# The scan's clamped decay differences: one subtraction on VectorE and one rectifier on ScalarE, or eight rectifiers with a bias on ScalarE

## The chip, the cores and the metric

One core of a Trainium2 chip runs the whole kernel. Times are device microseconds of that core; the median of the runs counts. TensorE multiplies matrices into PSUM, VectorE, ScalarE and GpSimd work element by element, and each engine works through a queue of its own in order. SyncE issues most of the DMAs.

## The reference

One step of a two-layer streaming encoder over 1024 prompt tokens and 32 sample tokens: first a Mamba-2 layer (SSD), then a latent attention layer, each followed by a gated per-layer embedding. What the change touches is in the scan of the first layer:

```python
Acs = jnp.cumsum(dt * A, axis=2)
seg = Acs[:, :, :, None] - Acs[:, :, None, :]
Lmat = jnp.exp(jnp.where(tri, seg, -jnp.inf))
CB = jnp.einsum('bclgn,bcsgn->bclsg', Cm, Bm)
M = CB[..., None] * Lmat * dt[:, :, None]
y_diag = jnp.einsum('bclsgr,bcsgrp->bclgrp', M, x)
```

`A` is negative, so `Acs` falls within a chunk, and `seg` is at most 0 wherever `tri` lets it through. There are 32 heads in 8 groups of 4.

## The kernel before, in words

The first layer (`phase_ssd`) goes by the 8 groups of heads. For each group six blocks of 128 columns of the input weights are multiplied with the normalised input (`mblock`, L311; the matmuls themselves are at L215 in `gemm`, with results in three PSUM buffers `mm`). The results go to SBUF through ScalarE (L327) or VectorE (L329), are convolved (L461 on ScalarE, three steps L463 on VectorE), and pass a SiLU (L188, L189). Every matrix is split into a high and a low part, so a product is three matmuls; ScalarE (L204) and GpSimd (L205) split the weights.

`scan_group` (L475) then runs over a group's tokens in five steps `q`: four quarters of the prompt with two chunks of 128 tokens each (the kernel uses chunks of 128, not 64), and the sample with one of 32. In a step:

- SyncE loads `ex` (L492): the running sums of four heads along the columns, the same on all partitions, [128, 4 heads, 256]. `ex` has two buffers. `eb` is loaded likewise (L495).
- TensorE transposes x and B into the PSUM tiles `trx` and `trb` (L500 to L502) and multiplies C and B into the other half of `trb` (L505). Each has one buffer.
- VectorE forms `xe` (L512) and `xd` (L518), ScalarE empties B out of `trb` into `bt` (L514), TensorE forms the chunk states `st` (L517), VectorE masks the products of C and B into `cbm` (L520), which lets `trb` go.
- The decays: VectorE subtracts from `ex` each row token's own sum `tok(32)` (L524), ScalarE forms max(0, -x) (L525) and exp(-x) (L526), VectorE multiplies with `cbm` (L527).
- VectorE and GpSimd carry the state `hT` from chunk to chunk (L535, L538, L540; three buffers), TensorE multiplies it with C into `yf` (L546) and `ex` with `xd` into `yd` (L553), and VectorE adds these up (L559 to L562) and adds the skip term (L566). The last state of the prompt and that of the sample are stored by ScalarE's queue (L488, L568).

`gate` (L467) multiplies the result of the group before with its gate on GpSimd (L473), `finish` (L570) normalises and stores it; the loop from L605 on writes scan, blocks and gates of neighbouring groups one after another. The order on the engines is not this one: the kernel is built under `tile.TileContext(nc, schedule_with_timeline_sim=True)` (L1522), a planner that orders every engine's queue at compile time by its own estimates of when each instruction can run, and that also sets the waits. So matmuls of a scan stand in between those of the next group's blocks.

Of the kernel before, what the change touches and what calls it, by code (L numbers as in the profile page):

```python
# [12 lines left out]
AF = mybir.ActivationFunctionType  # L13
ALU = mybir.AluOpType
# [158 lines left out]
def bc_last(ap, n):  # L173
    return ap.unsqueeze(len(ap.shape)).to_broadcast(list(ap.shape) + [n])
# [96 lines left out]
def phase_ssd(c, ctx):  # L271
    nc, tc, I, O = c.nc, c.tc, c.I, c.O
# [202 lines left out]
    def scan_group(g, S):  # L475
# [5 lines left out]
        for q in range(5):  # L481
            chs = (2 * q, 2 * q + 1) if q < 4 else (8,)
            nc_, L = (2, 128) if q < 4 else (1, 32)
# [7 lines left out]
            ex = wk.tile([P, 4, 256], F32, tag="ex", name="ex", bufs=2)[:L, :, :W]  # L491
# [15 lines left out]
            def tok(a):  # L507
                return tokT[:L, chs[0] : chs[0] + nc_, a + 4 * g : a + 4 * g + 4]
# [11 lines left out]
            nc.vector.tensor_tensor(cbm.rearrange("p (c l) -> p c l", c=nc_), trb[:L, :nc_, 128 : 128 + L],  # L520
                                    bc_mid(c.tri[:L, :L], nc_), op=ALU.mult)

            dv = ex.rearrange("p h (c l) -> p h c l", c=nc_)
            nc.vector.tensor_tensor(dv, dv, bc_last(tok(32).rearrange("p c h -> p h c"), L), op=ALU.subtract)  # L524
            nc.scalar.activation(ex, ex, AF.Relu, scale=-1.0)  # L525
            nc.scalar.activation(ex, ex, AF.Exp, scale=-1.0)  # L526
            nc.vector.tensor_tensor(ex, ex, bc_mid(cbm, 4), op=ALU.mult)  # L527
            yd = pc.tile([P, 2, 256], F32, tag="yd", name="yd")
# [76 lines left out]
    for g in range(G):  # L605
        scan_group(g, Ss[g])
        if g + 1 < G:
            bc_blocks(g + 1)
        if g:
            gate(g - 1, 0, Ss[g - 1])  # L610
            gate(g - 1, 1, Ss[g - 1])
        if g + 1 < G:
            x_block(g + 1, 0)
        else:
            gate(g, 0, Ss[g])
        if g:
            finish(g - 1, Ss[g - 1])
        if g + 1 < G:
            x_block(g + 1, 1)
        else:  # L620
            up = up_product(c, 0, (0, T), lambda: kp.tile([P, T1], F32, tag="cx", name="upr", bufs=6),
                            lambda: kp.tile([P, 3 + T1], F32R, tag="raw", name="upx", bufs=RAWB),
                            lambda: mm.tile([P, 512], F32, tag="mm", name="mm"),
                            lambda: kp.tile([P, T1], F32, tag="cx", name="upe", bufs=6), 4)
            next(up)
            gate(g, 1, Ss[g])
            finish(g, Ss[g])
# [908 lines left out]
```

## Time and profile before

| what | value |
|---|---|
| median of three runs | 2018.41 us (2017.17 to 2023.32) |
| the profiled execution's own time | 2016.99 us |
| its span from first to last instruction | 2015.2 us |
| mean granted TensorE clock | 0.992 of full speed (2.4 GHz) |
| TensorE, VectorE, ScalarE, GpSimd busy | 1931.1, 1301.3, 1003.1, 962.7 us |

The profile is of one execution. Busy time is the time in which an engine works on instructions; PE is TensorE's matmuls, PEld its weight loads, DVE VectorE, ACT ScalarE, POOL GpSimd, SPq the queue of SyncE's DMAs. "L524" is a line of the kernel. "[4.58 <-DVE ex L524]" behind an instruction says that its engine sat idle for 4.58 us just before it, and which instruction's end was the last that it waited for.

### The profile page before, as it was taken

What the parts mean: (1) busy time and instruction counts of PE and PEld (TensorE: products, weight loads), DVE (VectorE), ACT (ScalarE), POOL (GpSimd) and SP (SyncE); (2) the same over time, 40 slices, a digit from 0 to 9 for tenths busy, and PEclk for the clock granted to TensorE, in tenths of its full rate; (3) what the DMA queues carried; (4) which work ended last, traced back from release to release, by engine and by line L of the source; (5) the groups of instructions that cost most, each with busy time, mean ns of one, the idle gap of its engine ahead of it and who ended that gap; (6) DMA issues with size and microseconds to landing.
All of it is one profiled execution on the core that took longest, in us unless ns stands there. A gap on an engine that the chain in (4) does not pass through costs nothing. (4 is left out here: it accounts for less than half of the span.)

```text
span 2015.2 us, 32636 instructions
## 1 busy us (share of the span) xinstructions
PE 1931.1 (96%) x12867; PEld 1772.6 (88%) x12867; DVE 1301.3 (65%) x1646; ACT 1003.1 (50%) x1707; POOL 962.7 (48%) x811
## 2 busy tenths in 40 slices
PE   8999999999999998999998999999999999999999
PEld 6989899998999998999998899777778777779999
DVE  6889886758567675444267534264688787986444
ACT  4435444353444447333243441577687867754331
POOL 5543534343443444455678443122545453645773
PEclk9999999999999999999999999999999999999999
DMA  4133433324233336544333312433512221315432
GB/s 140 53 89 86 93 95 94 84 84 100 68 93 90 78 109 218 177 149 152 95 119 116 95 60 77 164 108 97 114 46 71 57 64 37 107 58 192 128 123 76
DMA packets 110730, 204.27 MB, mean 101 GB/s; under 512 B 18224, under 2 KB 60720, under 8 KB 110448
## 3 DMA queue, kind: packets, MB, share of 16 engines
q1 hardware_dynamic: 105472, 193.17, 32.7%
q0 software_dynamic: 2800, 6.91, 1.8%
q8 instruction: 101, 1.65, 0.3%
q10 hardware_dynamic: 2304, 2.10, 0.3%
q14 instruction: 53, 0.43, 0.1%
HBM read 156.81 MB, written 38.83 MB: 97 GB/s over the span
## 5 line engine op out<-in xcount | busy, mean ns | idle before, releaser
L205 POOL TENSOR_TENSOR wl<-wraw,wh 128x1024 fp32r<-128x1024 f32 (+2 forms) x185 | 376.4, 2036 | 459.9 <-ACT wh L204 416.9
L215 PE MATMUL mm<-hh,wh 128*128 128x384 f32 (+2 forms) x1152 | 376.9, 328 | 2.3 <-ACT xr L375 1.4
L215 PE MATMUL mm<-hh,wl 128*128 128x384 f32 (+2 forms) x1152 | 377.7, 328 | 0.0
L215 PE MATMUL mm<-hl,wh 128*128 128x384 f32 (+2 forms) x1152 | 376.1, 327 | 0.0
L204 ACT ACTIVATE wh<-wraw 128x1024 fp32r<-128x1024 f32 (+2 forms) x182 | 157.7, 866 | 265.8 <-PE pso L215 109.7
L215 PE MATMUL pso<-yhl,wh 128*128 128x264 f32 x1536 | 283.5, 285 | 5.9 <-DVE yhl L229 3.0
L215 PEld LDWEIGHTS pso<-yhl,wh 128*128 128x128 f32 x1536 | 239.6, 189 | 7.5 <-DVE yhl L229 4.0
L215 PE MATMUL pso<-yhl,wl 128*128 128x264 f32 x768 | 219.0, 285 | 2.5 <-POOL wl L205 2.5
L215 PEld LDWEIGHTS mm<-hh,wh 128*128 128x128 f32 (+1 forms) x1152 | 216.7, 188 | 5.3 <-ACT xr L375 1.7
L215 PEld LDWEIGHTS mm<-hh,wl 128*128 128x128 f32 (+1 forms) x1152 | 216.8, 188 | 4.2 <-issue 2.8
L215 PEld LDWEIGHTS mm<-hl,wh 128*128 128x128 f32 (+1 forms) x1152 | 216.9, 188 | 0.9 <-issue 0.2
L215 PE MATMUL psi<-yhl,wh 128*128 128x264 f32 (+1 forms) x896 | 166.2, 286 | 4.2 <-ACT yhl L228 3.9
L463 DVE SCALAR_TENSOR_TENSOR cx<-raw,pv,cx 128x1060 f32<-128x1060 f32 x96 | 141.7, 1480 | 39.3 <-ACT cx L461 38.6
L215 PEld LDWEIGHTS pso<-yhl,wl 128*128 128x128 f32 x768 | 145.1, 189 | 3.0 <-POOL wl L205 3.0
L215 PE MATMUL pg<-hH,wl 128*128 128x264 f32 x512 | 145.9, 285 | 0.6 <-POOL wl L205 0.6
L215 PE MATMUL pg<-hH,wh 128*128 128x264 f32 x512 | 145.9, 285 | 0.0
L215 PE MATMUL pg<-hL,wh 128*128 128x264 f32 x512 | 145.6, 285 | 0.0
L215 PEld LDWEIGHTS psi<-yhl,wh 128*128 128x128 f32 (+1 forms) x896 | 137.4, 184 | 5.9 <-ACT yhl L228 4.1
L1288 PE MATMUL st<-qk 128*128 128x512 f32 (+2 forms) x576 | 140.0, 358 | 1.2 <-DMA qk<-mr 0.5
L1309 POOL TENSOR_TENSOR pl<-pf,ph 128x512 fp32r<-128x512 f32 x64 | 81.5, 1273 | 106.8 <-DVE ph L1308 98.3
L215 PE MATMUL psi<-yhl,wl 128*128 128x264 f32 (+1 forms) x448 | 129.2, 288 | 1.6 <-POOL wl L205 1.6
L538 POOL TENSOR_TENSOR hm<-hT,cd_all 128x256 f32<-128x256 f32 x64 | 55.0, 859 | 136.5 <-DVE hT L540 83.3
(525 smaller groups left out, 4605.7 us busy)
## 6 DMA issues: line engine op xcount, KB each, us to landing
wraw<-in_inW SPq DMA_DIRECT2D x48, 512.0 KB, 3.5
ex<-acs_d SPq DMA_DIRECT2D x32, 512.0 KB, 5.3
wraw<-in_outW SPq DMA_DIRECT2D x32, 512.0 KB, 3.7
yraw<-y_d SPq DMA_DIRECT2D x32, 264.0 KB, 4.4
u<-u_d SPq DMA_DIRECT2D x32, 264.0 KB, 2.8
eb<-ea_d SPq DMA_DIRECT2D x64, 128.0 KB, 3.6
y_d<-y SPq DMA_DIRECT2D x16, 512.0 KB, 2.9
wraw<-in_gateW SPq DMA_DIRECT2D x16, 512.0 KB, 3.6
```

The lines of the kernel that those rows point to most:

```text
L204: nc.scalar.activation(wh, raw, AF.Copy)
L205: nc.gpsimd.tensor_tensor(wl, raw, wh.bitcast(F32), op=ALU.subtract)
L215: c.nc.tensor.matmul(ps, ww[:, k, :m], aa, start=first and k == 0 and i == 0, stop=last and k == n - 1 and i == 2)
L463: nc.vector.scalar_tensor_tensor(xh, raw[:, k : k + T1], pvc(c, "cw", 4 * b + k), xh, op0=ALU.mult, op1=ALU.add)
L538: nc.gpsimd.tensor_tensor(hm.rearrange("p (h q) -> p h q", q=64), hT.rearrange("p (h q) -> p h q", q=64), bc_last(cd_all[:, hs, ch], 64), ...
L1288: nc.tensor.matmul(ps[:, :n], a_[:, ks], b_[:, q], start=t == 0, stop=t == 2)
L1309: (nc.gpsimd if idx in L_POOL else nc.vector).tensor_tensor(pl[:, :n], pf[:, :n], ph[:, :n].bitcast(F32), op=ALU.subtract)
```

## The change

The subtraction L524 on VectorE goes. The rectifier L525 on ScalarE, one instruction over all of `ex`, becomes one for each head and chunk: eight a quarter, four for the sample, each over 128 (or 32) columns. Each takes the row tokens' own sums of its head and chunk, one number a partition, as its bias, so max(0, own sum - x) comes out in one go. Everything else stays as it was written.

```diff
-            dv = ex.rearrange("p h (c l) -> p h c l", c=nc_)
-            nc.vector.tensor_tensor(dv, dv, bc_last(tok(32).rearrange("p c h -> p h c"), L), op=ALU.subtract)
-            nc.scalar.activation(ex, ex, AF.Relu, scale=-1.0)
+            for h in range(4):
+                for i in range(nc_):
+                    e_ = ex[:, h, L * i : L * i + L]
+                    nc.scalar.activation(e_, e_, AF.Relu, scale=-1.0, bias=tok(32)[:, i, h : h + 1])
             nc.scalar.activation(ex, ex, AF.Exp, scale=-1.0)
             nc.vector.tensor_tensor(ex, ex, bc_mid(cbm, 4), op=ALU.mult)
```

## Rows read from the trace of the kernel before

**Rows 1.** The page's first part: the span, and each engine's busy time, its share of the span and its instructions.

```profile
span 2015.2 us, 32636 instructions
PE 1931.1 (96%) x12867; PEld 1772.6 (88%) x12867; DVE 1301.3 (65%) x1646; ACT 1003.1 (50%) x1707; POOL 962.7 (48%) x811
```

**Rows 2.** Busy time by stretches, in us from the span's start: length, then busy time and instructions of each engine, TensorE's granted clock, the DMA engines' share, GB/s. The second and third rows are the scan's stage and all that follows.

```profile
476.00:568.00 92.00, 89.22 (x607) 85.38 (x605) 63.94 (x76) 41.04 (x57) 36.74 (x40) 1.00 0.33 86
130.00:772.00 642.00, 623.25 (x4252) 592.37 (x4251) 467.90 (x567) 288.18 (x395) 264.15 (x264) 0.99 0.36 90
772.00:2015.00 1243.00, 1188.85 (x7929) 1071.63 (x7927) 728.18 (x971) 658.85 (x1223) 625.04 (x475) 0.99 0.36 109
```

**Rows 3.** Whom TensorE's matmuls waited for between 100 and 800 us: us in total, times, longest.

```profile
PE yd L553 <- DVE y L562: 4.6, 4, 1.7
PE trb L502 <- DVE cbm L520: 4.6, 5, 1.1
...
PE st L517 <- DVE hT L540: 3.2, 5, 0.7
...
PE yf L546 <- DVE hT L535: 1.7, 1, 1.7
PE psy L267 <- DVE y L562: 1.5, 1, 1.5
PE yf L546 <- DVE hT L540: 1.1, 1, 1.1
PE st L517 <- DVE xe L512: 1.0, 1, 1.0
...
PE psy L267 <- ACT ysh L228: 0.3, 1, 0.3
```

**Rows 4.** VectorE's instructions of the subtraction between 130 and 770 us, shapes kept apart: busy us, mean ns of one | idle time before them and what ended it.

```profile
L524 DVE TENSOR_TENSOR ex<-ex,tokT 128x1024 f32<-128x1024 f32 x32 | 53.0, 1657 | 23.7 <-DMA ex<-acs_d 23.7
L524 DVE TENSOR_TENSOR ex<-ex,tokT 32x128 f32<-32x128 f32 x8 | 2.2, 272 | 0.0
```

**Rows 5.** The same view for ScalarE: the rectifiers, and two instructions of the same shape with and without a bias from memory (`eps`).

```profile
L525 ACT ACTIVATE ex<-ex 128x1024 f32<-128x1024 f32 x32 | 33.9, 1061 | 77.5 <-DVE ex L524 77.5
...
L182 ACT ACTIVATE yr<-yr,eps 128x1060 f32<-128x1060 f32 x6 | 7.1, 1183 | 0.1
L183 ACT ACTIVATE yr<-yr 128x1060 f32<-128x1060 f32 x6 | 6.5, 1090 | 0.1
...
L525 ACT ACTIVATE ex<-ex 32x128 f32<-32x128 f32 x8 | 2.5, 308 | 25.8 <-DVE ex L524 25.8
```

**Rows 6.** What the view of the tile `ex` says of the subtraction (shortest, median and longest in ns, first and last start in us) and of the tile's DMA (shortest, median and longest us from issue to landing).

```profile
L524 DVE TENSOR_TENSOR ex<-ex,tokT x40: 271/1218/2999, 134.6 to 753.7; 128x1024 f32<-128x1024 f32 x32, 32x128 f32<-32x128 f32 x8
...
DMA to landing us min/median/max: 1.9/5.2/6.9
```

**Rows 7.** VectorE's timeline from 400 to 492 us, one group: start, us, the instruction, the idle time before it where there is any.

```profile
408.65 1.76 DVE L524 TENSOR_TENSOR ex<-ex,tokT 128x1024 f32<-128x1024 f32 x1 [2.93 <-DMA ex<-acs_d]
...
439.29 1.31 DVE L463 SCALAR_TENSOR_TENSOR cx<-raw,pv,cx 128x1060 f32<-128x1060 f32 x1
440.52 0.42 DVE L520 TENSOR_TENSOR cbm<-trb,cst 128x256 f32<-128x256 f32 x1
...
460.81 2.35 DVE L524 TENSOR_TENSOR ex<-ex,tokT 128x1024 f32<-128x1024 f32 x1
...
465.45 1.32 DVE L463 SCALAR_TENSOR_TENSOR cx<-raw,pv,cx 128x1060 f32<-128x1060 f32 x1 [1.63 <-ACT cx L461]
...
472.02 1.21 DVE L524 TENSOR_TENSOR ex<-ex,tokT 128x1024 f32<-128x1024 f32 x1
...
482.37 1.24 DVE L189 SCALAR_TENSOR_TENSOR raw<-zs,raw 128x1060 f32<-128x1060 f32 x1
...
486.81 0.42 DVE L540 TENSOR_TENSOR hT<-hm,st 128x256 f32<-128x256 f32 x1
487.14 0.68 DVE L559 TENSOR_TENSOR eb<-yf,eb 128x512 f32<-128x512 f32 x1
```

**Rows 8.** ScalarE's timeline in the same stretch.

```profile
458.22 0.40 ACT L327 ACTIVATE raw<-mm 128x292 f32<-128x292 f32 x1
463.19 1.06 ACT L525 ACTIVATE ex<-ex 128x1024 f32<-128x1024 f32 x1 [4.58 <-DVE ex L524]
464.15 1.26 ACT L461 ACTIVATE cx<-raw,pv 128x1060 f32<-128x1060 f32 x1
465.32 1.04 ACT L526 ACTIVATE ex<-ex 128x1024 f32<-128x1024 f32 x1
466.27 0.36 ACT L514 ACTIVATE bt<-trb 128x256 f32<-128x256 f32 x1
```

**Rows 9.** The timelines of GpSimd and TensorE from 480 to 494 us, the end of the same group's scan.

```profile
483.69 2.46 POOL L473 TENSOR_TENSOR y<-y,raw 128x1060 f32<-128x1060 f32 x1 [2.03 <-DVE raw L189]
486.11 0.67 POOL L538 TENSOR_TENSOR hm<-hT,cd_all 128x256 f32<-128x256 f32 x1
...
487.28 0.69 PE L517 MATMUL st<-xe,bt 32*128 32x256 f32 x2 [0.65 <-DVE hT L540]
...
493.16 0.42 PE L553 MATMUL yd<-ex,xd 32*64 32x32 f32 x8 [1.08 <-DVE y L562]
```

**Rows 10.** Whom ScalarE (first two rows) and VectorE waited for between 100 and 800 us: us in total, times, longest.

```profile
ACT ex L525 <- DVE ex L524: 103.3, 37, 5.5
...
ACT raw L327 <- DVE hT L540: 48.8, 7, 9.0
...
DVE ex L524 <- DMA ex<-acs_d: 23.7, 11, 2.9
```

## The prediction, made before the change was run

> **What bounds the kernel.** I read the page's busy times first: TensorE is busy for 96% of the span, VectorE 65%, ScalarE 50% [rows 1]. An average over stages says little about one edit, so next came the table by stretches. The edited lines run from 130 to 770 us. In 130 to 772 us TensorE is busy for 623.25 of 642 us, VectorE for 467.90 (73%) and ScalarE for 288.18 (45%); in the even group from 476 to 568 us TensorE leaves 2.8 us of 92 [rows 2]. So TensorE's own work sets the time here, and nothing that is done on VectorE or ScalarE counts except through TensorE's 18.75 us of idleness. Whatever the change gives must come out of these.
>
> The third view is who TensorE waits for. Nearly all of it is VectorE: y L562, cbm L520 and hT L540 come first, with 4.6, 4.6 and 3.2 us, then single waits [rows 3]. None is for `ex`: the lines that the diff edits never hold TensorE directly. They act only as something that stands in front of other work in VectorE's queue and in ScalarE's.
>
> **The change, part by part.** *VectorE loses L524.* 32 subtractions of 1024 columns and 8 of 128, 53.0 and 2.2 us [rows 4]: 55.2 us, which leaves 467.9 - 55.2 = 412.7 us (64%). They are slow on average, 1657 ns, against a median of 1218 and a longest of 2999 [rows 4, 6].
>
> *ScalarE loses 40 rectifiers and gets 288.* The old ones take 1061 ns (1024 columns) and 308 ns (128 columns) [rows 5]. No row shows 128 x 128 with a bias from memory, so I bound it. The 128-column rectifier of 308 ns has the right width; a bias from memory adds 93 ns (L182, which has one, 1183, L183, which has none, 1090, same 1060 columns) [rows 5]; together 401 ns. Consecutive ScalarE instructions without a dependence overlap by about 0.09 us (463.19 + 1.06 is 464.25, the next starts at 464.15; 464.15 + 1.26 is 465.41, the next starts at 465.32) [rows 8]. The eight pieces don't depend on each other. So a quarter costs 8 x 0.311 + 0.09 = 2.58 us, or 3.21 us if nothing overlaps; the old one cost 1.06, so 1.52 to 2.15 us more. For the sample's 32 columns: (1061 - 308) / 896 = 0.84 ns a column, 308 - 96 x 0.84 + 93 = 320 ns, four of them 1.01 to 1.28 us against 0.31. A group of four quarters and one sample then costs 4 x 1.52 + 0.70 = 6.8 us more (upper bound 9.6), eight groups 54 us (77). I take the lower value, as the overlap is in the rows. ScalarE rises to 342 us of 642 (53%; 57% at the upper bound), which still has cover under TensorE's 97%.
>
> *The wait moves.* The rectifier no longer waits for VectorE (103.3 us over 37 waits) but for the DMA of `ex`, for which L524 waited 23.7 us over 11 [rows 10]. That transfer lands 5.2 us after its issue [rows 6]. Before, ScalarE sat behind DMA and VectorE together; after, behind the DMA alone, so the wait can only end sooner. Queued behind it on ScalarE are the evictions L327 and L514. SyncE's queue gets nothing new. The bare chain of a quarter stays as long: 1.22 to 1.66 us plus 1.06 before, 2.58 after. What changes is the place in the queues.
>
> *What that is worth, in one group.* From 465.45 to 487.8 us VectorE runs without a gap, so there it is late, and it starts late: L463 at 465.45 sat idle for 1.63 us until ScalarE's L461, which was queued behind the rectifier at 463.19, which had waited 4.58 us for L524 at 460.81 (2.35 us long) [rows 7, 8]. After the change ScalarE is free at 458.62 and the data are there at 460.81 at the latest (L524 shows no wait for them), so the eight pieces end between 461.2 and 463.4 and L461 starts 0.8 to 2.9 us earlier. L463 can follow, since L524's 2.35 us have also gone from ahead of it. Further on L524 at 472.02, 1.21 us, goes too [rows 7]. Together VectorE's gate product L189 at 482.37 comes 2.0 to 4.1 us earlier. On it hangs a chain: GpSimd's L473 at 483.69, L538 behind it at 486.11, VectorE's L540 at 486.81, TensorE's L517 at 487.28, which waited 0.65 us; then by the state's store and L562 the matmul L553 at 493.16, which waited 1.08 us [rows 7, 9]. Both waits are shorter than 2.0 us, so both can go. Over all groups these two kinds are 3.2 and 4.6 us [rows 3]: at most 7.8 us.
>
> Not reached are the waits of L502 for cbm L520 (4.6 us): at 440.52 cbm stands behind a convolution step at 439.29, and no L524 runs between 411 and 460 us [rows 7]. The first group's xe and hT L535 (1.0 and 1.7 us) and psy (1.5 us) have no L524 directly ahead either.
>
> *The sum.* The bounds of the gain are 0 and 7.8 us. The planner sets every engine's order anew from its own costs, so the matmuls of the scan will not stand where they stood; what is left of a wait is the difference between its plan and the chip. I take half: 3.9 us. The profiled execution took 2016.99 us (span 2015.2 and 1.8 around it), so 2013.1 by its measure; it lies 1.4 us below the median of the runs, 2018.41, and I forecast medians: 2014.5 us, with 2010.6 to 2018.4 as the range of this case alone.
>
> **A rule that speaks against it.** Rows: one whole-tile pass of 1024 columns is 1218 ns on VectorE and 1061 ns on ScalarE, but eight pieces with their own biases are 2.58 us by the working above [rows 5, 6]. The Trainium skill (ScalarE: Activation LUTs, Rules for kernel authors) says that relu, max and add belong on VectorE and not on ScalarE. For the whole tile the trace does not agree; cut into eight it does. By this rule the change would lose, and how it would lose here is the rival below that ends slower.
>
> **The rivals.** *Nothing is gained.* The planner moves the matmuls up as VectorE's work comes earlier, and the same leftovers of about a microsecond reappear elsewhere. For it: the wait sizes repeat from group to group as a plan's errors would. Against: some of VectorE's lateness comes from instructions that took longer than their usual time (2.35 and 1.76 us instead of 1.22), and fewer of these are left. Time: 2018.4, within 3 us.
>
> *Nearly all of TensorE's waits go.* With 55 us less, VectorE is no longer late anywhere: the waits on it from 130 us on in [rows 3] (4.6, 4.6, 3.2, 1.7, 1.5, 1.1, 1.0) make 17.7 us; three quarters or so of them gives 13, 2005 us. Against: the cbm waits above.
>
> *Slower: ScalarE holds bt back.* L514 empties the one bank trb, and cbm and the next transposes need it. If L514 stands behind a run of eight, it comes 1.52 us later. At 466.27 it stands right behind the pair for `ex` [rows 8]; once a group, and TensorE has no slack at trb (five waits of L502 show that [rows 3]). Price: 8 x 1.52 = 12.2 us, 2030.6 us. It decides from the point where the slack between bt and the next transposes is under 1.5 us. Against: L327 on the same queue bears waits of up to 9.0 us [rows 10] and TensorE waits for ScalarE hardly at all in this stage [rows 3]; ScalarE's long waits for VectorE go too.
>
> *The later stage is planned differently.* After 772 us TensorE is idle for 1243.0 - 1188.85 = 54 us [rows 2]. If the new order there wins or loses a sixth of it: 9 us either way.
>
> **How the numbers follow.** A measurement of this kernel tells about 0.3% (6 us) from no change: faster is under 2012.4 us, slower over 2024.5. Chances: forecast 0.45, nothing gained 0.17, nearly all 0.18, slower by ScalarE 0.12, later stage 0.08 (half each way). Faster: a fifth of the forecast's own range lies under 2012.4 (0.10), with 0.18 and 0.04: 0.32. Same: 0.35 + 0.17 = 0.52. Slower: 0.12 + 0.04 = 0.16. The range of 8 in 10 takes in most of the 13 us gain and the near half of a loss: 2003 to 2026 us.
>
> **What would show it.** Right: VectorE in 130 to 772 us near 413 us; pieces of 128 columns near 0.40 us; a run of eight near 2.6; TensorE's waits for hT L540 and y L562 halved or better, those for cbm still there; TensorE's busy time unchanged. Wrong: new waits of TensorE for bt, for mm's eviction or for ScalarE's `ex`; pieces well over 0.4 us; other idle times after 772 us that outweigh those before it.

## The result, and the profile after

The changed kernel takes 2006.67 us (median of five, 2002.14 to 2008.34) against 2018.41 us: the ratio is 0.9934, 95% interval 0.9911 to 0.9956. So it is faster by 0.7%, some 12 us. Its profiled execution took 2008.34 us, with a span of 2006.6.

Busy time by stretches, as in [rows 2] (length, TensorE, its weight loads, VectorE, ScalarE, GpSimd, clock, DMA share, GB/s). The first row is the same 92 us as there, the second the whole stretch.

```profile
476.00:568.00 92.00, 91.86 (x623) 88.23 (x623) 59.75 (x78) 48.41 (x93) 36.40 (x40) 1.00 0.33 86
130.00:772.00 642.00, 632.81 (x4323) 603.19 (x4322) 419.31 (x532) 344.47 (x658) 260.55 (x269) 1.00 0.38 94
```

TensorE leaves 0.1 us of the group's 92 idle, where it left 2.8. VectorE lost 49 us in the long stretch and ScalarE gained 56. Where the first layer ends is seen in the last matmul of its blocks (tile `mm`: count, shortest, median, longest ns, first and last start). The kernel before:

```profile
L215 PE MATMUL mm<-hh,wl x1152: 291/334/669, 33.2 to 774.3; 128*128 128x384 f32 x139, 128*128 128x292 f32 x48, 128*32 128x384 f32 x3, 128*32 128x292 f32 x2
```

The changed one:

```profile
L215 PE MATMUL mm<-hh,wl x1152: 292/334/669, 34.7 to 762.7; 128*128 128x384 f32 x139, 128*128 128x292 f32 x48, 128*32 128x384 f32 x3, 128*32 128x292 f32 x2
```

From the transposes ahead of the scan (L449, 127.6 us before and 129.1 after) to this matmul the stage took 646.7 us and takes 633.6: 13.1 us less, which is more than the 8.6 us by which the spans of these two executions differ. From there to the end it is 1240.9 and 1243.9 us, and the way to the scan took 1.5 us longer. The stage in the view by stretches, before and after:

```profile
127.50:774.50 647.00, 628.18 (x4282) 597.32 (x4283) 470.40 (x570) 288.91 (x396) 267.45 (x270) 0.99 0.36 90
```

```profile
129.00:762.90 633.90, 626.16 (x4282) 596.99 (x4283) 416.86 (x530) 335.43 (x644) 255.95 (x270) 1.00 0.37 92
```

So of the 13.1 us some 11 are TensorE's idle time (18.8 to 7.7 us) and 2 its busy time, for the same 4282 matmuls; the mean granted clock of the stage was 0.99 and 1.00 of full speed (2.4 GHz).

Whom TensorE waited for between 100 and 800 us, as in [rows 3]:

```profile
...
PE yf L547 <- DVE hT L536: 1.7, 1, 1.7
PE trb L502 <- DVE cbm L520: 1.3, 1, 1.3
PE yd L554 <- DVE ex L528: 1.2, 2, 0.8
...
PE st L517 <- DVE xe L512: 0.9, 1, 0.9
...
PE yf L547 <- DVE hT L541: 0.7, 2, 0.5
```

The waits for the state (st, 3.2 us) and for y (yd 4.6, psy 1.5) have gone, that for cbm fell from 4.6 to 1.3. New is one of 1.2 us for `ex` (L528). In all, TensorE waits 6.3 us for VectorE between 127 and 770 us, against 16.6. ScalarE's new pieces between 130 and 762 us, and a run of eight and one of four in its timeline:

```profile
L526 ACT ACTIVATE ex<-ex,tokT 128x128 f32<-128x128 f32 x256 | 79.4, 389 | 120.1 <-DMA ex<-acs_d 120.1
```

```profile
469.74 2.45 ACT L526 ACTIVATE ex<-ex,tokT 128x128 f32<-128x128 f32 x8 [5.47 <-DMA ex<-acs_d]
472.22 1.06 ACT L527 ACTIVATE ex<-ex 128x1024 f32<-128x1024 f32 x1
...
477.47 0.95 ACT L526 ACTIVATE ex<-ex,tokT 32x32 f32<-32x32 f32 x4 [2.69 <-DMA ex<-acs_d]
```

### The profile page after: what moved, and what is told of

Same layout as the page of the kernel before. It is cut to its first block, busy times and chain, and to the rows that moved or that the text cites. A ratio compares the mean times of both kernels' runs of the same rounds, so it can differ in the third digit from the quotient of the medians.

```text
span 2006.6 us, 32822 instructions
## 1 busy us (share of the span) xinstructions
PE 1934.6 (96%) x12867; PEld 1775.7 (88%) x12867; DVE 1250.9 (62%) x1606; ACT 1049.7 (52%) x1955; POOL 952.7 (47%) x811
## 5 line engine op out<-in xcount | busy, mean ns | idle before, releaser
L205 POOL TENSOR_TENSOR wl<-wraw,wh 128x1024 fp32r<-128x1024 f32 (+2 forms) x185 | 371.6, 2010 | 445.8 <-ACT wh L204 423.5
L526 ACT ACTIVATE ex<-ex,tokT 128x128 f32<-128x128 f32 (+1 forms) x288 | 87.0, 380 | 136.1 <-DMA ex<-acs_d 132.7
```

Source lines behind the costliest of these rows:

```text
L205: nc.gpsimd.tensor_tensor(wl, raw, wh.bitcast(F32), op=ALU.subtract)
L526: nc.scalar.activation(e_, e_, AF.Relu, scale=-1.0, bias=tok(32)[:, i, h : h + 1])
```

## The experiments

The theories, as they are numbered below (no kernel has the number e6). **1**: VectorE's 55 us were what counted. **2**: ScalarE no longer stands behind VectorE. **3**: any new order of the planner would have done it. **4**, formed after e8: the kernel before lost its time in the state's update, which waits for a store, and the change's order lost that wait.

The table gives every kernel's median, its ratio to the kernel before on the same chip, its scan stage as measured above, and TensorE's waits for VectorE between 127 and 770 us in its profile.

| kernel | us | ratio (95%) | stage, us | waits, us |
|---|---|---|---|---|
| before | 2018.41 | 1 | 646.7 | 16.6 |
| changed | 2006.67 | 0.9934 (0.9911 to 0.9956) | 633.6 | 6.3 |
| e1 VectorE's time back, behind a DMA | 2029.26 | 1.0074 (1.0060 to 1.0088) | 658.0 | 25.5 |
| e2 before, subtraction on GpSimd | 2014.25 | 0.9987 (0.9975 to 0.9999) | 642.9 | 13.9 |
| e3 changed, ScalarE's pieces doubled | 2002.44 | 0.9935 (0.9921 to 0.9948) | 632.9 | 5.1 |
| e4 changed, pieces in other order | 2003.12 | 0.9940 (0.9928 to 0.9952) | 635.1 | 6.0 |
| e5 VectorE's time back, no wait | 2012.62 | 0.9989 (0.9978 to 1.0001) | 640.5 | 13.2 |
| e7 before, rectifier in eight | 2005.40 | 0.9949 (0.9930 to 0.9968) | 632.2 | 6.1 |
| e8 before, four state buffers | 2003.40 | 0.9940 (0.9920 to 0.9959) | 635.6 | 10.3 |
| e9 before, no subtraction | 2002.69 | 0.9936 (0.9917 to 0.9955) | 628.5 | 5.6 |
| e10 before, stores on GpSimd's queue | 2006.88 | 0.9954 (0.9936 to 0.9971) | 634.7 | 9.4 |
| e11 changed, four state buffers | 2002.58 | 0.9938 (0.9916 to 0.9959) | 632.2 | 5.0 |
| e12 e5's kind, four state buffers | 2020.53 | 1.0020 (1.0007 to 1.0033) | 649.1 | 19.3 |
| e13 before, rectifier in two | 2014.35 | 0.9988 (0.9974 to 1.0002) | 643.9 | 11.9 |

Over all fourteen the stage is long where TensorE waits long for VectorE: every kernel with under 11 us of waits has a stage of 628 to 636 us, and every one above 11 us a stage over 640. Each row is one profiled execution, and the two columns going together says where the time is lost, not what causes it.

**e1, VectorE's time put back.**

```diff
+            for d in range(2):
+                jk = wk.tile([P, 2, 256], mybir.dt.bfloat16, tag="jk", name="jk")[:L, :, :W]
+                nc.vector.tensor_tensor(jk..., eb[:L]..., bc_last(tok(32)[:, :, 2 * d : 2 * d + 2]..., L), op=ALU.subtract)
```

> The changed kernel, with VectorE's time put back: after the rectifiers VectorE subtracts the same sums from eb, twice 512 columns a quarter, into a scratch tile that nobody reads. ScalarE does not wait for these. Theory 1 (VectorE's time was what counted): the gain is lost, 2013 to 2020 us, and TensorE waits for VectorE's cbm, hT and y again by over 10 us between 130 and 770 us. Theory 2 (what counted is that ScalarE no longer stands behind VectorE): the gain stays, 2003 to 2010 us. Theory 3 (only the new order counted): any value between.

2029.26 us: more than the gain is lost. But the work added stood in VectorE's queue for a DMA, as its waits show (us in total, times, longest):

```profile
DVE jk L529 <- DMA eb<-ea_d: 73.7, 37, 5.3
```

So it shows that a wait in VectorE's queue costs, and does not tell busy time from waiting. e5 does.

**e2, VectorE relieved by GpSimd.**

```diff
-            nc.vector.tensor_tensor(dv, dv, bc_last(tok(32)...), op=ALU.subtract)
+            nc.gpsimd.tensor_tensor(dv, dv, bc_last(tok(32)...), op=ALU.subtract)
```

> The kernel before, with the subtraction L524 on GpSimd: VectorE loses the same 55 us, ScalarE keeps one rectifier and now waits for GpSimd. Theory 1 (VectorE's time): 2002 to 2012 us, if GpSimd's some 2 us apiece do not make its own work late. Theory 2 (ScalarE's wait): no gain, 2014 to 2024 us, as ScalarE stands behind a slower engine than before. Theory 3 (order): 2010 to 2024 us.

2014.25 us, a gain of 0.1%. VectorE is relieved as in the change (413 us), but GpSimd takes 1.9 us apiece (median) and is now late with its part of the state: VectorE waits 20.8 us for L538, against 8.4 before. Not decisive: it took work from one engine on the state's path and gave it to another on the same path.

**e3, ScalarE's pieces doubled.**

```diff
                     nc.scalar.activation(e_, e_, AF.Relu, scale=-1.0, bias=tok(32)[:, i, h : h + 1])
+                    nc.scalar.activation(e_, e_, AF.Copy)
```

> The changed kernel, with a copy of each piece onto itself right behind its rectifier: 288 more instructions on ScalarE of about 0.3 us, 75 to 90 us, which takes it to two thirds of the scan's stage. My theory (ScalarE has room in this stage): within 4 us of the changed kernel, 2003 to 2011 us. Rival (ScalarE's time holds bt and the evictions back, which the change only just avoided): 2015 us or more, with new waits of TensorE for cbm behind bt.

Ratio 0.9935, the same as the change. The 256 larger copies take 296 ns each, and ScalarE is busy for 392 of the 632 us from 130 to 762 us:

```profile
130.00:762.00 632.00, 625.28 (x4279) 595.76 (x4278) 419.18 (x528) 391.57 (x934) 266.84 (x265) 1.00 0.37 92
```

The rival that ended slower is refuted: ScalarE has room for twice what the change gave it. TensorE's order differs here from the changed kernel's and the time does not, so the gain does not hang on one lucky order either.

**e4, the pieces in the other order.**

```diff
-            for h in range(4):
-                for i in range(nc_):
+            for i in range(nc_):
+                for h in range(4):
```

> The changed kernel with the eight pieces in the other order, chunk by chunk and not head by head; the same work on every engine. Theories 1 and 2: within 2 us of the changed kernel. Theory 3 (the gain is a lucky order of the planner): a value that differs by 4 us or more, either way.

0.9940, as the change. But TensorE's order came out the same, row by row, so it says nothing on theory 3. It is worth something else: from the blocks' last matmul to the end it takes 1237.9 us in its profile, the changed kernel 1243.9, with the same order. The 3.0 us that the change seems to lose after its stage are less than that.

**e5, VectorE's time put back without a wait.**

```diff
+            for d in range(2):
+                jk = wk.tile([P, 2, 256], mybir.dt.bfloat16, tag="jk", name="jk")[:L, :nc_]
+                nc.vector.tensor_tensor(jk, xd, xe, op=ALU.subtract)
```

> The changed kernel with VectorE's time put back as in e1, but on data that VectorE itself has just made (xd and xe, 512 columns, twice a quarter, into a scratch tile that nobody reads), so that nothing is waited for. e1 lost more than the gain, but its added work stood for 73.7 us in VectorE's queue until eb had landed. Theory 1a (VectorE's busy time counts): 2011 to 2019 us, the gain lost. Theory 1b (what counts is that VectorE's queue no longer stands behind a DMA): 2002 to 2008 us, the gain stays.

2012.62 us, 0.9989: five sixths of the gain are lost, as theory 1a has it. But two things speak against reading it so. Somewhat more was put back than the change took out: over the stage VectorE is busy for 478 us, against 470 in the kernel before and 417 in the changed one. And one more thing is back in VectorE's waits, the update of the state waiting for its store:

```profile
DVE hT L544 <- DMA out_ssm_o<-hT: 6.7, 3, 2.9
```

**e7, ScalarE's part alone.**

```diff
-            nc.scalar.activation(ex, ex, AF.Relu, scale=-1.0)
+            for h in range(4):
+                for i in range(nc_):
+                    e_ = ex[:, h, L * i : L * i + L]
+                    nc.scalar.activation(e_, e_, AF.Relu, scale=-1.0)
```

> The kernel before, subtraction on VectorE kept, with its rectifier cut into the eight pieces (four for the sample) of the change, without a bias: ScalarE's part of the change alone. All theories: no gain, as VectorE loses nothing. Theory 1: within 5 us of before, 2012 to 2022 us, ScalarE's added some 45 us being hidden. Rival (ScalarE's time costs something that the change's gain covers): 2022 us or more. Theory 3 (any new order helps): under 2010 us.

2005.40 us, 0.9949. No theory that needed VectorE's relief expected this: the subtraction is still on VectorE, ScalarE has more to do, and the kernel is as fast as the change. Theory 2 falls as well, since ScalarE still waits 91.9 us for L524. Of the expectations only theory 3's had room for it.

**e8, a fourth buffer for the state.**

```diff
-                    hT = wk.tile([P, 256], F32, tag="hT", name="hT0", bufs=3)
+                    hT = wk.tile([P, 256], F32, tag="hT", name="hT0", bufs=4)
...
-                hN = wk.tile([P, 256], F32, tag="hT", name="hT", bufs=3)
+                hN = wk.tile([P, 256], F32, tag="hT", name="hT", bufs=4)
```

> The kernel before with four buffers instead of three for the state hT, so that the state's update does not wait for its store (17.3 us over 4 waits of VectorE before, none after the change). If TensorE's waits for y L562 (4.6 us) came from that store and not from VectorE's time: 2011 to 2014 us and no such waits. Theory 1: not over 2 us of gain, 2014 to 2019 us.

2003.40 us, 0.9940: the same gain as the change's, with nothing moved. Here the orders on VectorE and ScalarE are the same as in the kernel before, and TensorE's differs at one pair of matmuls, so the two profiles can be laid side by side. The end of one group's scan on VectorE, before:

```profile
486.81 0.42 DVE L540 TENSOR_TENSOR hT<-hm,st 128x256 f32<-128x256 f32 x1
487.14 0.68 DVE L559 TENSOR_TENSOR eb<-yf,eb 128x512 f32<-128x512 f32 x1
492.08 0.42 DVE L540 TENSOR_TENSOR hT<-hm,st 128x256 f32<-128x256 f32 x1 [4.25 <-DMA out_ssm_o<-hT]
492.42 0.68 DVE L562 TENSOR_TENSOR y<-yd,eb 128x512 f32<-128x512 f32 x1
```

and with four buffers:

```profile
483.73 0.42 DVE L540 TENSOR_TENSOR hT<-hm,st 128x256 f32<-128x256 f32 x1
484.07 0.68 DVE L559 TENSOR_TENSOR eb<-yf,eb 128x512 f32<-128x512 f32 x1
486.41 0.42 DVE L540 TENSOR_TENSOR hT<-hm,st 128x256 f32<-128x256 f32 x1 [1.66 <-POOL hm L538]
486.75 0.68 DVE L562 TENSOR_TENSOR y<-yd,eb 128x512 f32<-128x512 f32 x1
```

Between the two updates lay 5.27 us, of which 4.25 were a wait for the prompt's state to land in HBM; now it is 2.68 us. Behind that update stood y L562, for which TensorE's yd waited (4.6 us, now 1.4), and on ScalarE the store's issue, behind which the eviction L327 stood ([rows 10], 48.8 us, now 14.2). TensorE's wait for cbm, well into the next group, fell as well, from 4.6 to 1.6 us. The places agree: in the kernel before the update waits for its store in four groups (at 400, 492, 584 and 677 us), yd's four waits come about 1 us behind these, and three of the five waits for cbm 40 us behind the first three. TensorE's waits of st for the state hardly changed (3.2 to 2.8 us), so those do not come from the store.

**e9, no subtraction.**

```diff
-            dv = ex.rearrange("p h (c l) -> p h c l", c=nc_)
-            nc.vector.tensor_tensor(dv, dv, bc_last(tok(32)...), op=ALU.subtract)
```

> The kernel before without the subtraction L524 (the decays are then those of the running sums alone: this part of the computation is left out), with one rectifier. VectorE is relieved as in the change, ScalarE gets nothing new. Theory 1: as fast as the changed kernel within 3 us, 2000 to 2009 us; what it is faster by is the price of ScalarE's pieces. Theory 3: any value between 2000 and 2020 us.

0.9936. VectorE's relief without any price on ScalarE is worth just what the change is worth, so the eight pieces cost nothing that the runs can tell.

**e10, the stores on another queue.**

```diff
-                nc.scalar.dma_start(O["ssm_o"]...
+                nc.gpsimd.dma_start(O["ssm_o"]...
```

> The kernel before with the two stores of the state (L488, L568) issued by GpSimd's queue and not by ScalarE's. Theory 4a (what the kernel before lost is ScalarE's queue: the eviction L327 stood for 48.8 us behind the stores' issue): 2002 to 2009 us. Theory 4b (what it lost is the state's update L540, which waits until the store has landed, 17.3 us, and with it y, the next group's ex and TensorE's yd): no gain or a loss, 2011 to 2022 us, with that wait still there.

0.9954, as 4a has it. But the wait of L540 for the store, which 4b expected to stay, has gone too: the update waits almost only for GpSimd's hm. At the end of the group shown in e8 it starts at 485.45 us, 1.8 us behind the issue of the prompt's store at 483.69, sooner than any of this kernel's stores landed (2.2 us at the least): here it does not wait for the landing at all, and why is not shown. The orders on VectorE and TensorE in this stage are those of the kernel before. So e10 confirms the place (the two stores and what stands behind them) and does not tell the two ways apart. e8 does in part: there the stores are still on ScalarE's queue, and the gain is the same; but ScalarE's wait behind them fell there too.

**e11, the change and the fourth buffer together.**

> The changed kernel with four buffers for the state hT, as in e8. Theory 4 (the change and e8 removed the same wait): no further gain, within 3 us of the changed kernel, 2000 to 2008 us. Theory 1 (VectorE's time is a gain of its own, beside the store's): the two add up, 1988 to 1997 us.

0.9938. The change alone gives 0.9934, the buffer alone 0.9940, both together no more, as theory 4 has it: the two gains do not add up. How the changed kernel is rid of the wait is seen on VectorE at the end of the same group:

```profile
484.27 0.42 DVE L541 TENSOR_TENSOR hT<-hm,st 128x256 f32<-128x256 f32 x1 [0.52 <-POOL hm L539]
...
485.68 0.68 DVE L563 TENSOR_TENSOR y<-yd,eb 128x512 f32<-128x512 f32 x1
486.39 2.54 DVE L567 SCALAR_TENSOR_TENSOR y<-cx,pv,y 128x1024 f32<-128x1024 f32 x2
489.45 0.42 DVE L541 TENSOR_TENSOR hT<-hm,st 128x256 f32<-128x256 f32 x1 [0.52 <-POOL hm L539]
```

The update at 489.45 comes 4.7 us behind the store's issue at 484.73, as it did before (492.08 behind 487.26, 4.8 us). But y and the skip term, which stood behind the update, now stand ahead of it, so nothing idles while the store lands, and y comes 1.4 us behind the update at 484.27 and not 5.6. It is so in all four groups in which the update waited before, here and in e9. So the time between store and update is as long as it was; the planner's order has filled it with other work.

**e12, VectorE's time back, with the fourth buffer.**

```diff
+            for d in range(4):
+                jk = wk.tile([P, 256], mybir.dt.bfloat16, tag="jk", name="jk")[:L]
+                nc.vector.tensor_tensor(jk, xd[:, d % nc_], xe[:, d % nc_], op=ALU.subtract)
```

> The changed kernel with VectorE's time put back on data of its own (four subtractions of 256 columns a step, xd less xe, into a scratch tile that nobody reads; some 1.3 to 1.6 us a quarter) and with four buffers for the state. e5, with three buffers, lost most of the gain (2012.6 us), and the state's update waited for its store again (6.7 us). Theory 4 (VectorE's time costs only through that wait): 2000 to 2007 us. Theory 1 (VectorE's time costs by itself): 2010 to 2018 us.

2020.53 us, 1.0020. Theory 4 in that form falls: no update waits for a store here, and VectorE's added time costs all the same. But half as much again as the change took out was put back: over the stage VectorE is busy for 498 us, 27 more than in the kernel before. So this prices more work on VectorE than the 55 us. TensorE now waits for the state itself, and VectorE's timeline shows why:

```profile
488.70 2.65 DVE L529 TENSOR_TENSOR jk<-xd,xe 128x256 bf16<-128x256 f32 x1
491.29 0.40 DVE L544 TENSOR_TENSOR hT<-hm,st 128x256 f32<-128x256 f32 x1
```

```profile
491.74 0.71 PE L550 MATMUL yf<-cx,hT 128*128 128x128 f32 x4 [2.54 <-DVE hT L544]
```

The planner put a piece of the added work directly ahead of the state's update. Its median is 0.42 us; this one took 2.65, while GpSimd ran L473 from 488.65 to 491.08, and TensorE stood still for 2.54 us. Such waits for hT come to 14.0 us.

**e13, the rectifier in two.**

```diff
-            nc.scalar.activation(ex, ex, AF.Relu, scale=-1.0)
+            for h in range(0, 4, 2):
+                nc.scalar.activation(ex[:, h : h + 2], ex[:, h : h + 2], AF.Relu, scale=-1.0)
```

> The kernel before, subtraction kept, with its rectifier cut into two pieces of two heads each: some 7 us more on ScalarE and nothing else, but enough for the planner to set a new order on TensorE. Theory 3 (nearly any new order loses the wait that the order before had): 2000 to 2009 us. Theory 1: 2013 to 2021 us. Theory 4: as fast as e8 where the state's update no longer waits for its store, as slow as before where it does.

2014.35 us, 0.9988. TensorE's order is new and the kernel is hardly faster, so not any new order will do. VectorE's waits:

```profile
DVE hT L541 <- POOL hm L539: 18.7, 9, 4.2
DVE hT L541 <- DMA out_ssm_o<-hT: 8.2, 2, 4.7
```

The state's update is late again, and TensorE waits 5.3 us for y behind it.

## Why the prediction was right or wrong

**Right: the direction, the range, and the place.** TensorE sets the time, its busy time hardly changed (1931.1 and 1934.6 us), and nearly all of the gain is its idle time in the scan's stage, where it had waited for VectorE. The range of 2003 to 2026 held 2006.67, but only because it took in the rivals: the range of this case alone, 2010.6 to 2018.4, did not.

**Right: the costs.** A piece takes 389 ns (forecast 401), a run of eight 2.45 us (2.58), a sample's four 0.95 us (1.01). VectorE has 419 us from 130 to 772 us (413; the stretch now holds 9 us of the stage that follows), ScalarE 344 (342). The wait moved to ScalarE, with 132.7 us for the DMA of `ex`, and it made TensorE late only in the first group: there yd waited 0.8 and 0.4 us for L528, which had itself waited 4.1 and 2.1 us for ScalarE's exp behind the pieces. That is one of the signs named under "Wrong", at a tenth of the gain. The rival by the rule of the Trainium skill (ScalarE: Activation LUTs, Rules for kernel authors) did not come about: e3 shows that in this stage twice as much on ScalarE is still free, and e9 that the pieces have no price that the runs can tell.

**Wrong: the size.** I forecast 3.9 us; it was 11.7 by the medians. Two terms of the sum fail. First the halving: I kept half of 7.8 us because the planner would leave some of it. The waits for hT at st and for y at yd went entirely, all 7.8 us. Second the sentence "Not reached are the waits of L502 for cbm L520": they fell by 3.3 us, and psy's 1.5 us went. Together these are 12.6 us, about the gain. I had looked only for an L524 directly ahead of cbm. e8 shows that these waits hang on the end of the group before, since one buffer there takes them from 4.6 to 1.6 us. The rival "nearly all of TensorE's waits go", 2005 us, is what happened, though its reason, 55 us less on VectorE, is not shown to be the cause.

**Wrong: the cause.** I put the lateness at the end of a group down to VectorE's unbroken work from 465 to 488 us, and passed over "the state's store" in half a sentence. It was a term of its own: the update at 492.08 waited 4.25 us for that store, and not for VectorE. e8 removes this wait alone and gains the same; e11 shows that it and the change don't add up. So it was not needed to relieve VectorE of its 55 us: e7, e8 and e10 keep all of them and are as fast. Nor is VectorE's time free: work that brings it to 7 and 27 us above the kernel before costs the changed kernel 0.5 and 0.9% (e5, e12), in e12 where it lands ahead of the state's update. What e1 to e13 agree on is narrower than theory 1: the stage is long where TensorE waits for the state, y or cbm in VectorE's queue. In the changed kernel these waits are short; for y by an order in which it no longer stands behind the update that waits for the store (e11), for the state perhaps by what was taken out of that queue, as the prediction's chain had it, which no run tests alone.

**Open.** How the gain divides between VectorE's time and the order. e8 and e10 take the store's wait away with the order of the kernel before and gain as much as the change, so that wait is enough to explain the gain; but no run takes VectorE's time away within that order, so what it is worth alone is not known. And why e7 is as fast as it is: its update still waits 10.4 us for the store in four waits, though TensorE waits only 6.1 us for VectorE; its new order seems to keep TensorE fed over that wait, but which exchange of instructions does it was not tried.

## What to carry to other kernels

Where one engine sets the time and a planner orders the rest, do not price an edit by the work it moves: look up whom the bounding engine waits for, follow each wait back to its first cause, across queues and from one group into the next, and try that cause alone. Here a fourth buffer of 1 KB a partition for a tile that is being stored gave the same as moving 55 us of work between engines. And an engine that is busy for less than three quarters of a stage can still be the one that is late, if short steps of a chain through it stand behind long ones.

## What the runs showed of the hardware

A short VectorE instruction can take several times as long beside GpSimd: 0.42 us in the median, 2.65 us while GpSimd ran L473 (e12). In the changed kernel the same is seen at L528, whose shortest is 0.27 us:

```profile
479.90 2.35 DVE L528 TENSOR_TENSOR ex<-ex,cbm 32x128 f32<-32x128 f32 x1 [0.27 <-ACT ex L527]
```

```profile
479.75 2.36 POOL L205 TENSOR_TENSOR wl<-wraw,wh 128x1024 fp32r<-128x1024 f32 x1 [1.39 <-ACT wh L204]
```

They end at 482.25 and 482.11 us, as if the small one had to wait for the large one's end. The Trainium skill (GPSIMD Engine Reference, Specifications) says that the two share their interfaces to SBUF, with contention for VectorE instructions of two SBUF inputs; these have two, and the trace agrees. An instruction with one input in SBUF and one in PSUM was not stretched: in the kernel before, L540 at 477.74 took 0.40 us while GpSimd ran L205 from 477.65 to 480.07, and L189 right behind it, with two SBUF inputs, 3.11 us against 1.26 at other times. That the small one is held for nearly the whole length of GpSimd's instruction is read from these places alone.

ScalarE showed no such stretching: the pieces lie between 302 and 405 ns over all 288, and a bias from memory costs the same 93 ns on them as in [rows 5] (389 against 296 ns in e3 and 297 in e7).
